# A two-layer decoder trunk: a wider stationary operand in the block MLP, and the DeltaNet coupling product cut to its 64x64 chunk

## The chip, the cores and the metric

One core of one Trainium2 chip. The metric is device microseconds of the whole program, the median over runs. Engines are named as the profile names them: PE is TensorE (PEld its weight loads, which run beside it), DVE is VectorE, ACT is ScalarE, POOL is GpSimd, and SP is SyncE, whose queue issues most DMAs. A product here is one matmul call of the kernel: `out = lhsT.T @ rhs`, with `lhsT` the stationary operand (loaded into the array) and `rhs` the moving one.

## The reference, cut to what matters

The reference is a trunk of two layers on 256 tokens of width 2048, batch 1. Layer 0 mixes tokens with NSA attention and retention, layer 1 with a gated DeltaNet; both go on with cross-attention into 256 memory tokens and a SwiGLU FFN. The change touches two places.

In layer 0, keys and values of NSA's compressed branch come from an MLP over overlapping blocks of 32 tokens (15 blocks, two groups):

```python
def compress_blocks(t, pos, w1, w2):
    ...
    blocks = blocks + pos[None, None, :, None, :].astype(t.dtype)
    flat = blocks.transpose(0, 3, 1, 2, 4).reshape(b, g, n_cmp, NSA_CMP_LEN * dh)
    return jax.nn.silu(flat @ w1) @ w2
```

`flat` has 30 rows (15 blocks by 2 groups) of 32 times 128 values, `w1` is 4096 by 256, `w2` is 256 by 128. It is done twice, for keys and for values.

In layer 1, each of 32 heads solves a unit lower triangular system per chunk of 64 tokens, and the state passes from chunk to chunk:

```python
def chunk_gated_delta_rule(q, k, v, beta, g):
    ...
    lower = jnp.where(strict, jnp.einsum('bhncd,bhnmd->bhncm', kb, k) * decay, 0.0)
    ...
    sol = lax.linalg.triangular_solve(lower + jnp.eye(C, dtype=f32), rhs, left_side=True,
                                      lower=True, unit_diagonal=True)
```

## The kernel before, in words

**Exact products from two parts.** The large products don't run in plain fp32. Weights and activations are each split into a high part (rounded to the fp32r type by a copy on ScalarE) and a low part (the rest, by a subtraction on VectorE), and three products with fp32r operands are added up: high by high, high by low, low by high (`passes`, line 232). A weight tile of 512 KB is loaded by SP into one of four buffers (`load_weight`, line 218) and split in pieces of 512 columns by lines 214 and 215. The products of all projections and of the block MLP are issued from line 237.

**Order of the work.** The kernel is one straight program. Projections run in the foreground; everything else (attention heads, the block MLP, the triangular inverses, the solves) are generator tasks. After every six products of a projection a counter advances by one (`tick`, line 112), and each task whose waiting time is over issues its next piece; `yield n` waits `2 n` ticks. So the interleaving is written out by hand in the number of projection products between two pieces of a task. The tile framework then fixes each engine's order once, ahead of the run.

**The block MLP** (`compress`, line 858, spawned twice by `nsa_keys`, for keys and values). It adds the position terms to windows of the projected tokens (tile `cf`), splits the result into `cfh` and `cfl` of 32 by 30 columns, and then for each of the 32 token positions multiplies by that position's 128 rows of `w1`: the 30 columns are stationary, 256 weight columns move, three products per position, 96 per branch, into 30 partitions of one PSUM bank (`cmp`). Both branches run between the products of the NSA query projections, so that SP's queue brings one tile of projection weights and two of block weights in turn. Afterwards silu is taken on the 30 partitions (three activations and a multiplication), two transposes (line 888) turn it, two copies (line 891) bring it to SBUF, and the second layer follows (lines 895 and 906).

**The DeltaNet solves** (`solver`, line 1383; `pair` and `head` in it, spawned by `gdn_inputs` for 16 key heads with two value heads each). The inverses of all 64x64 triangles are worked out ahead (`invert`, line 1311), go through DRAM by 16 stores of SP (line 1355), and come back by `pair` (line 1398) as block-diagonal tiles `bd` of 128 by 128: two chunks of 64 tokens at once, in two buffers that are filled with zeros once (line 1387). With 256 tokens a head has two such halves, t = 0 and 1. In `head`:

- `M` holds the decayed key scores of both halves and between them; `bv` holds beta times v.
- Line 1437, two products per head: the transposed inverses times the scores within a half, 128 by 128 times 128 by 128, give the coupling of the second chunk to the first; one copy on ScalarE (line 1439) puts both halves into the tile `nT`. `clear` (in `gdn_inputs`) has set the scores within a half to zero but for rows 0 to 63 and columns 64 to 127, so the result is zero outside that block.
- Line 1448, per half: `nT` (stationary) times `bv` (moving), which VectorE subtracts with a decay factor (line 1449); line 1451: the inverses times the result; line 1452: a copy to `u`. Line 1445 couples the halves.
- Lines 1454 to 1456 form the output; it is normalised and gated into `nT` again (line 1465), transposed (line 1470) and stored in `R` (line 1474).

All these products have plain fp32 operands. They run in between projections of values and the output projection, by the same ticks (`HOP` is 1).

Of the kernel before, what the change touches and what calls it, by code (L numbers as in the profile page):

```python
# [10 lines left out]
F32 = mybir.dt.float32  # L11
F32R = mybir.dt.float32r
AF = mybir.ActivationFunctionType
ALU = mybir.AluOpType
# [4 lines left out]
P = 128  # L19
# [59 lines left out]
def trunk(ctx: ExitStack, tc: tile.TileContext, a: dict, out: bass.AP, phases=ALL):  # L79
    nc = tc.nc  # L80
    V, S, G, PE = nc.vector, nc.scalar, nc.gpsimd, nc.tensor
# [55 lines left out]
    def give(n):  # L137
        state["banks"] += n
# [6 lines left out]
    ident = gp.tile([P, P], F32, name="ident")  # L145
# [72 lines left out]
    def load_weight(W, k0, nk, c0, ncol, g=None):  # L218

        w = wp.tile([P, nk, ncol], F32, tag="w", name="w")  # L220
        state["load"] = nc.sync.dma_start(w, W[k0 * P : (k0 + nk) * P, c0 : c0 + ncol].rearrange("(k p) c -> p k c", p=P))
        n = max(1, 512 // ncol)
        parts = []
        if g is not None:
            n = 1
        for k in range(0, nk, n):
            m = min(n, nk - k)
            h, l = split_weight(w[:, k : k + m, :], g and g(k0 + k))
            parts += [(h[:, i, :], l[:, i, :]) for i in range(m)]
        return parts  # L230

    def passes(o, x, w, start, last, x_stationary=False):

        (xh, xl), (h, l) = x, w
        pairs = ((xh, h), (xh, l), (xl, h)) if x_stationary else ((h, xh), (h, xl), (l, xh))
        for j, (s_, m) in enumerate(pairs):
            PE.matmul(o, s_, m, start=start and j == 0, stop=last and j == 2, skip_group_check=True)  # L237
# [153 lines left out]
    def sigmoid_(dst, src):  # L391

        S.activation(dst, src, AF.Exp, scale=-1.0)
        S.activation(dst, dst, AF.Ln, bias=c_one[: dst.shape[0]])
        S.activation(dst, dst, AF.Exp, scale=-1.0)
# [462 lines left out]
    def compress(ck, br, kvT, kcat, vc):  # L858

        f = ck.tile([P, 32, 30], F32, tag="cf", name="cf")  # L860
        for g in range(2):
            src = kvT[:, 2 * br + g, :]
            win = bass.AP(src.tensor, src.offset, [list(src.ap[0]), [1, 32], [16, 15]])
            pos = small[:, 17 + 32 * br : 17 + 32 * (br + 1)]
            V.tensor_add(f[:, :, g * 15 : (g + 1) * 15], win, pos[:, :, None].to_broadcast([P, 32, 15]))
        fh = ck.tile([P, 32, 30], F32R, tag="cfh", name="cfh", bufs=2)
        fl = ck.tile([P, 32, 30], F32R, tag="cfl", name="cfl", bufs=2)
        S.activation(fh, f, AF.Copy)
        V.tensor_sub(fl, f, fh.bitcast(F32))
        w2 = ck.tile([P, 2, P], F32, tag="cw2", name="cw2", bufs=2)  # L870
        S.dma_start(w2, a["nsa_cmp_w2"][0, br].rearrange("(j p) c -> p j c", p=P))
        W1 = a["nsa_cmp_w1"][0, br]
        yield from take(1)
        b = bank("cmp")
        ph = b[:30, 0:256]
        for k0 in range(0, 32, 4):
            for k, w in enumerate(load_weight(W1, k0, 4, 0, 256)):
                kk = k0 + k
                passes(ph, (fh[:, kk, :], fl[:, kk, :]), w, kk == 0, kk == 31, True)
                if k % 2:  # L880
                    yield 1
        sg = ck.tile([30, 256], F32, tag="csg", name="csg", bufs=2)
        hs = ck.tile([30, 256], F32, tag="chs", name="chs", bufs=2)
        sigmoid_(sg, ph)
        V.tensor_mul(hs, ph, sg)
        yield 2
        for j in range(2):
            PE.transpose(b[:, 256 + j * 32 : 256 + j * 32 + 30], hs[:, j * P : (j + 1) * P], ident[:30, :30])
        hT = ck.tile([P, 2, 30], F32, tag="chT", name="chT", bufs=2)
        for j in range(2):  # L890
            V.tensor_copy(hT[:, j, :], b[:, 256 + j * 32 : 256 + j * 32 + 30])
        yield 1
        if br == 0:
            for j in range(2):
                PE.matmul(b[:, 0:30], w2[:, j, :], hT[:, j, :], start=j == 0, stop=j == 1)
            kr = ck.tile([P, 30], F32, name="kr")
            V.tensor_copy(kr, b[:, 0:30])
            give(1)
            kn = ck.tile([P, 30], F32, name="kn")
            yield from head_rms(kr, kg[:, 0:1], kn, n=30)  # L900
            for g in range(2):
                V.tensor_copy(kcat[:, g, 512:527], kn[:, g * 15 : (g + 1) * 15])
        else:
            for g in range(2):
                for j in range(2):
                    PE.matmul(
                        b[:15, g * P : (g + 1) * P], hT[:, j, g * 15 : (g + 1) * 15], w2[:, j, :],
                        start=j == 0 and g == 0, stop=j == 1, skip_group_check=True,
                    )
                V.tensor_copy(vc[:15, g, :], b[:15, g * P : (g + 1) * P])  # L910
            give(1)
# [471 lines left out]
    def solver(gs, R, d_T, d_rows, neg, colD, beta, negc, rq, mhalf):  # L1383

        bds = [gs.tile([P, 2, 2, 2, P], F32, name=f"bd{j}", bufs=1) for j in range(2)]
        for bd in bds:
            G.memset(bd, 0.0)
        gcol = small[:, 16:17]

        def pair(q, vT, z, before):  # L1390
# [20 lines left out]
        def head(h, j, vT, z, bd, gb, begun):  # L1411
            yield from take(1)
            q = h // 2
            m = gs.tile([P, 384], F32, tag="M", name="M")
# [9 lines left out]
            b = bank("slv")  # L1424
            zc = (h % 4) * P
# [8 lines left out]
                S.activation(bv[:, t, :], b[:, 256 + t * P : 256 + (t + 1) * P], AF.Copy, scale=col(beta, t))  # L1434
            yield 1
            for t in range(2):
                PE.matmul(b[:, t * P : (t + 1) * P], bd[:, j, t, 0, :], m[:, 2 * t * P : 2 * t * P + P], start=True, stop=True)  # L1437
            nT = gs.tile([P, 2, P], F32, tag="nT", name="nT")
            S.activation(nT, b[:, 0:256].rearrange("p (t c) -> p t c", t=2), AF.Copy)
            yield HOP  # L1440
            u = gs.tile([P, 2, P], F32, tag="u", name="u")
            for t in range(2):
                rhs = bv[:, t, :]
                if t:
                    PE.matmul(b[:, 0:P], m[:, P:256], u[:, 0, :], start=True, stop=True)  # L1445
                    V.scalar_tensor_tensor(rhs, b[:, 0:P], col(negc, 1), rhs, ALU.mult, ALU.add)
                    yield HOP
                PE.matmul(b[:, 256:384], nT[:, t, :], rhs, start=True, stop=True)  # L1448
                V.scalar_tensor_tensor(rhs, b[:, 256:384], col(negc, t), rhs, ALU.mult, ALU.add)
                yield HOP  # L1450
                PE.matmul(b[:, 384:512], bd[:, j, t, 1, :], rhs, start=True, stop=True)  # L1451
                S.activation(u[:, t, :], b[:, 384:512], AF.Copy)
                yield HOP
# [9 lines left out]
            V.tensor_mul(st[:, 2:4], st[:, 2:4], rq[:, :, h])  # L1463
            for t in range(2):
                V.scalar_tensor_tensor(
                    nT[:, t, :], b[:, t * P : (t + 1) * P], st[:, 2 + t : 3 + t], z[:, t, zc : zc + P], ALU.mult, ALU.mult
                )
            yield 2 * HOP
            for t in range(2):
                PE.transpose(b[:, 256 + t * P : 256 + (t + 1) * P], nT[:, t, :], ident)  # L1470

            while len(begun) < 2:
                yield 1
# [53 lines left out]
```

## Time and profile before

| | |
|---|---|
| time, median of 3 runs | 3032.07 us (3030.87 to 3035.57) |
| the profiled execution | 3029.89 us |
| its span, first to last instruction | 3028.1 us |
| PE busy | 2962.2 us (98%), 22981 products' records |
| PEld busy | 2839.1 us (94%) |
| DVE busy | 2034.9 us (67%) |
| ACT busy | 1698.0 us (56%) |
| POOL busy | 111.9 us (4%) |
| DMA | 568.56 MB, mean 188 GB/s |
| PE's granted clock, mean | 0.991 |

Times are microseconds from the span's start unless marked ns. PE's records are pipelined: a product's duration reaches into the next one's, so what a product costs is read from the distance of starts, not from its duration. A row of the timeline gives start, length, engine, line, operation, `out<-in`, the shape, and how many instructions are merged into it; `30*128` means 30 rows (partitions of the contraction) by 128 columns of the stationary operand, `128x256` what moves. In brackets stands idle time of that engine ahead of the row and who ended it; "issue" is a release that the profile doesn't show.

### The profile page before, as it was taken

To read this page: it belongs to the slowest core of one execution; us is meant where nothing else is said; L and a number is where in the kernel's file an instruction comes from. 1 tells how busy PE (TensorE), PEld (TensorE's weight loads), DVE (VectorE), ACT (ScalarE), POOL (GpSimd) and SP (SyncE) were. 2 spreads that over 40 slices of the span, in tenths; PEclk is the share of its full clock that TensorE was granted. 3 is DMA by queue.
4 is the path that set the end of the run, shared out by engine and by line. 5 is a ranking of instruction groups with operands and counts; after the bars stand their busy time and mean duration, and the time that the engine had idled before them with its cause. 6 is when DMAs were issued, how large, how long until landed. Compare 5 with 4: busy or idle time off the path is not lost.

```text
span 3028.1 us, 59625 instructions
## 1 busy us (share of the span) xinstructions
PE 2962.2 (98%) x22981; PEld 2839.1 (94%) x22981; DVE 2034.9 (67%) x3879; ACT 1698.0 (56%) x3316; POOL 111.9 (4%) x153
## 2 busy tenths in 40 slices
PE   9999999999999999999989959999999999999999
PEld 8899899999999999999978959999999999999887
DVE  6867676675666665567689948886667566655554
ACT  6655655665555554456655637776556554545444
POOL 0000000000000000000110100122000000000000
PEclk9999999999999999999999989999999999999999
DMA  7775555566666665566777557564556666665664
GB/s 242 204 235 168 154 147 174 181 182 195 193 196 190 195 195 195 195 196 183 195 223 229 173 145 200 164 173 132 192 183 182 194 194 190 187 188 182 199 197 167
DMA packets 339547, 568.56 MB, mean 188 GB/s; under 512 B 43661, under 2 KB 83653, under 8 KB 339133
## 3 DMA queue, kind: packets, MB, share of 16 engines
q1 hardware_dynamic: 333376, 550.79, 61.2%
q0 software_dynamic: 2576, 7.82, 0.9%
q10 hardware_dynamic: 3308, 6.14, 0.7%
q8 instruction: 180, 2.95, 0.4%
q14 instruction: 107, 0.87, 0.1%
HBM read 549.16 MB, written 13.93 MB: 186 GB/s over the span
## 4 chain that ended last, share of the span: by engine, by line
PE 95%; DVE 2%; DMA 2%; SPq 1%; ACT 1%; issue 0%; POOL 0%; DVEq 0%; ACTq 0%; POOLq 0%
PE pj L237 87%; SPq L1355 1%; PE cmp L237 1%; DMA w<-in_hyb_w_in 1%; DVE w_lo L215 1%; PE slv L1451 0%; PE slv L1448 0%; PE slv L1437 0%; DMA w<-in_gdn_w_in 0%; DVE xT L424 0%; DMA d_T<-AB 0%; DVE x_lo L357 0%; PE slv L1445 0%; DMA mraw<-in_mem 0%; PE kk L1065 0%
## 5 line engine op out<-in xcount | busy, mean ns | idle before, releaser
L215 DVE TENSOR_TENSOR w_lo<-w,w_hi 128x512 fp32r<-128x512 f32 x1938 | 1329.6, 692 | 862.7 <-ACT w_hi L214 847.6
L214 ACT ACTIVATE w_hi<-w 128x512 fp32r<-128x512 f32 x1938 | 1217.1, 631 | 1141.0 <-DVE w_lo L215 589.8
L237 PE MATMUL pj<-x_hi,w_hi 128*128 128x256 f32 (+1 forms) x4496 | 1247.0, 280 | 36.5 <-ACT w_hi L214 36.1
L237 PE MATMUL pj<-x_lo,w_hi 128*128 128x256 f32 x4496 | 1246.1, 279 | 0.0
L237 PE MATMUL pj<-x_hi,w_lo 128*128 128x256 f32 (+1 forms) x4496 | 1226.0, 280 | 1.2 <-DVE w_lo L215 1.2
L237 PEld LDWEIGHTS pj<-x_hi,w_hi 128*128 128x128 f32 (+1 forms) x4496 | 848.2, 189 | 39.2 <-ACT w_hi L214 37.5
L237 PEld LDWEIGHTS pj<-x_lo,w_hi 128*128 128x128 f32 x4496 | 845.2, 188 | 1.1 <-issue 0.2
L237 PEld LDWEIGHTS pj<-x_hi,w_lo 128*128 128x128 f32 (+1 forms) x4496 | 831.4, 188 | 3.0 <-DVE w_lo L215 2.2
L237 PE MATMUL pj<-hl,w_hi 128*128 128x256 f32 x704 | 193.7, 276 | 0.0
L237 PE MATMUL pj<-hh,w_hi 128*128 128x256 f32 x704 | 193.6, 276 | 0.0
L237 PE MATMUL pj<-hh,w_lo 128*128 128x256 f32 x704 | 192.4, 276 | 0.0
L237 PE MATMUL pj<-o,w_hi 128*128 128x256 f32 x1024 | 184.8, 283 | 2.0 <-ACT o L1007 1.6
L237 PE MATMUL pj<-w_lo,x_hi 128*128 128x512 f32 (+2 forms) x448 | 172.1, 385 | 3.5 <-DVE w_lo L215 3.5
L237 PE MATMUL pj<-w_hi,x_lo 128*128 128x512 f32 (+2 forms) x448 | 169.5, 379 | 0.0
L237 PEld LDWEIGHTS pj<-o,w_hi 128*128 128x128 f32 x1024 | 157.3, 191 | 2.8 <-ACT o L1007 2.1
L237 PE MATMUL pj<-w_hi,x_hi 128*128 128x512 f32 (+2 forms) x448 | 142.6, 384 | 4.4 <-ACT w_hi L214 4.4
L237 PE MATMUL pj<-o,w_lo 128*128 128x256 f32 x512 | 142.3, 282 | 0.0
L237 PE MATMUL pj<-w_hi,hl 128*128 128x512 f32 x352 | 138.3, 393 | 0.0
L237 PE MATMUL pj<-w_lo,hh 128*128 128x512 f32 x352 | 137.7, 391 | 0.0
L237 PEld LDWEIGHTS pj<-hl,w_hi 128*128 128x128 f32 x704 | 132.2, 188 | 0.0
L237 PEld LDWEIGHTS pj<-hh,w_hi 128*128 128x128 f32 x704 | 132.2, 188 | 0.0
L237 PEld LDWEIGHTS pj<-hh,w_lo 128*128 128x128 f32 x704 | 131.3, 188 | 0.0
(414 smaller groups left out, 3621.7 us busy)
## 6 DMA issues: line engine op xcount, KB each, us to landing
w<-in_ffn_w_in SPq DMA_DIRECT2D x352, 512.0 KB
w<-in_gdn_w_in SPq DMA_DIRECT2D x193, 512.0 KB
w<-in_ffn_w_out SPq DMA_DIRECT2D x176, 512.0 KB
w<-in_hyb_w_in SPq DMA_DIRECT2D x96, 512.0 KB
w<-in_gdn_w_out SPq DMA_DIRECT2D x64, 512.0 KB
w<-in_xa_wkv SPq DMA_DIRECT2D x32, 512.0 KB
w<-in_hyb_w_out SPq DMA_DIRECT2D x32, 512.0 KB
w<-in_nsa_cmp_w SPq DMA_DIRECT2D x16, 512.0 KB
```

What stands on the lines that cost most here:

```text
L214: state["hi"] = S.activation(h, w, AF.Copy)
L215: V.tensor_sub(l, w, h.bitcast(F32))
L237: PE.matmul(o, s_, m, start=start and j == 0, stop=last and j == 2, skip_group_check=True)
L1355: nc.sync.dma_start(bass.AP(dst.tensor, dst.offset, [[64 * 512, 8], [512, 64], [1, 128]]), AB[p0 : p0 + 15 : 2].rearrange("p i w j -> p i ...
```

## The change

The block MLP puts high and low part side by side into one tile `cfp` of 60 columns per position. One product with the high weights then does both parts at once (60 partitions of PSUM), and one of 30 columns with the low weights adds to the first 30: two products per position instead of three. The two halves of the result are added only after the transposes, and silu is taken there, on 128 partitions by 60 elements. The evacuation is reordered with it.

In the solves, the coupling product takes only the 64 rows and 64 columns that matter: the first chunk's inverse and the scores from the first chunk to the second. Its result goes into columns 64 to 127 of one of four fixed tiles `ns` of 64 partitions, filled with zeros once; the product with it (line 1448) contracts over 64 partitions instead of 128. The tile `nT` is gone; the gated output goes into `bv`.

```diff
@@ -863,33 +863,35 @@
             win = bass.AP(src.tensor, src.offset, [list(src.ap[0]), [1, 32], [16, 15]])
             pos = small[:, 17 + 32 * br : 17 + 32 * (br + 1)]
             V.tensor_add(f[:, :, g * 15 : (g + 1) * 15], win, pos[:, :, None].to_broadcast([P, 32, 15]))
-        fh = ck.tile([P, 32, 30], F32R, tag="cfh", name="cfh", bufs=2)
-        fl = ck.tile([P, 32, 30], F32R, tag="cfl", name="cfl", bufs=2)
-        S.activation(fh, f, AF.Copy)
-        V.tensor_sub(fl, f, fh.bitcast(F32))
+
+        fp = ck.tile([P, 32, 60], F32R, tag="cfp", name="cfp", bufs=2)
+        S.activation(fp[:, :, 0:30], f, AF.Copy)
+        V.tensor_sub(fp[:, :, 30:60], f, fp.bitcast(F32)[:, :, 0:30])
         w2 = ck.tile([P, 2, P], F32, tag="cw2", name="cw2", bufs=2)
         S.dma_start(w2, a["nsa_cmp_w2"][0, br].rearrange("(j p) c -> p j c", p=P))
         W1 = a["nsa_cmp_w1"][0, br]
         yield from take(1)
         b = bank("cmp")
-        ph = b[:30, 0:256]
         for k0 in range(0, 32, 4):
-            for k, w in enumerate(load_weight(W1, k0, 4, 0, 256)):
+            for k, (h, l) in enumerate(load_weight(W1, k0, 4, 0, 256)):
                 kk = k0 + k
-                passes(ph, (fh[:, kk, :], fl[:, kk, :]), w, kk == 0, kk == 31, True)
+                PE.matmul(b[:60, 0:256], fp[:, kk, :], h, start=kk == 0, stop=kk == 31, skip_group_check=True)
+                PE.matmul(b[:30, 0:256], fp[:, kk, 0:30], l, start=False, stop=kk == 31, skip_group_check=True)
                 if k % 2:
                     yield 1
-        sg = ck.tile([30, 256], F32, tag="csg", name="csg", bufs=2)
-        hs = ck.tile([30, 256], F32, tag="chs", name="chs", bufs=2)
-        sigmoid_(sg, ph)
-        V.tensor_mul(hs, ph, sg)
+        hs = ck.tile([60, 256], F32, tag="chs", name="chs", bufs=2)
+        S.activation(hs, b[:60, 0:256], AF.Copy)
+        yield 1
+        for j in range(2):
+            PE.transpose(b[:, 256 + j * 64 : 256 + j * 64 + 60], hs[:, j * P : (j + 1) * P], ident[:60, :60])
+        bt = b[:, 256:384].rearrange("p (j c) -> p j c", j=2)
+        hT = ck.tile([P, 2, 30], F32, tag="chT", name="chT", bufs=2)
+        sg = ck.tile([P, 2, 30], F32, tag="csg", name="csg", bufs=2)
+        V.tensor_copy(hT, bt[:, :, 0:30])
+        V.tensor_add(hT, hT, bt[:, :, 30:60])
+        sigmoid_(sg, hT)
+        V.tensor_mul(hT, hT, sg)
         yield 2
-        for j in range(2):
-            PE.transpose(b[:, 256 + j * 32 : 256 + j * 32 + 30], hs[:, j * P : (j + 1) * P], ident[:30, :30])
-        hT = ck.tile([P, 2, 30], F32, tag="chT", name="chT", bufs=2)
-        for j in range(2):
-            V.tensor_copy(hT[:, j, :], b[:, 256 + j * 32 : 256 + j * 32 + 30])
-        yield 1
         if br == 0:
             for j in range(2):
                 PE.matmul(b[:, 0:30], w2[:, j, :], hT[:, j, :], start=j == 0, stop=j == 1)
@@ -1385,6 +1387,10 @@
         bds = [gs.tile([P, 2, 2, 2, P], F32, name=f"bd{j}", bufs=1) for j in range(2)]
         for bd in bds:
             G.memset(bd, 0.0)
+
+        ns = [gs.tile([64, 2, P], F32, name=f"ns{j}", bufs=1) for j in range(4)]
+        for n in ns:
+            G.memset(n, 0.0)
         gcol = small[:, 16:17]
 
         def pair(q, vT, z, before):
@@ -1434,9 +1440,12 @@
                 S.activation(bv[:, t, :], b[:, 256 + t * P : 256 + (t + 1) * P], AF.Copy, scale=col(beta, t))
             yield 1
             for t in range(2):
-                PE.matmul(b[:, t * P : (t + 1) * P], bd[:, j, t, 0, :], m[:, 2 * t * P : 2 * t * P + P], start=True, stop=True)
-            nT = gs.tile([P, 2, P], F32, tag="nT", name="nT")
-            S.activation(nT, b[:, 0:256].rearrange("p (t c) -> p t c", t=2), AF.Copy)
+                PE.matmul(
+                    b[0:64, t * 64 : (t + 1) * 64], bd[0:64, j, t, 0, 0:64], m[0:64, 2 * t * P + 64 : 2 * t * P + P],
+                    start=True, stop=True,
+                )
+            n = ns[h % 4]
+            S.activation(n[:, :, 64:128], b[0:64, 0:128].rearrange("p (t c) -> p t c", t=2), AF.Copy)
             yield HOP
             u = gs.tile([P, 2, P], F32, tag="u", name="u")
             for t in range(2):
@@ -1445,7 +1454,7 @@
                     PE.matmul(b[:, 0:P], m[:, P:256], u[:, 0, :], start=True, stop=True)
                     V.scalar_tensor_tensor(rhs, b[:, 0:P], col(negc, 1), rhs, ALU.mult, ALU.add)
                     yield HOP
-                PE.matmul(b[:, 256:384], nT[:, t, :], rhs, start=True, stop=True)
+                PE.matmul(b[:, 256:384], n[:, t, :], rhs[0:64, :], start=True, stop=True)
                 V.scalar_tensor_tensor(rhs, b[:, 256:384], col(negc, t), rhs, ALU.mult, ALU.add)
                 yield HOP
                 PE.matmul(b[:, 384:512], bd[:, j, t, 1, :], rhs, start=True, stop=True)
@@ -1463,11 +1472,11 @@
             V.tensor_mul(st[:, 2:4], st[:, 2:4], rq[:, :, h])
             for t in range(2):
                 V.scalar_tensor_tensor(
-                    nT[:, t, :], b[:, t * P : (t + 1) * P], st[:, 2 + t : 3 + t], z[:, t, zc : zc + P], ALU.mult, ALU.mult
+                    bv[:, t, :], b[:, t * P : (t + 1) * P], st[:, 2 + t : 3 + t], z[:, t, zc : zc + P], ALU.mult, ALU.mult
                 )
             yield 2 * HOP
             for t in range(2):
-                PE.transpose(b[:, 256 + t * P : 256 + (t + 1) * P], nT[:, t, :], ident)
+                PE.transpose(b[:, 256 + t * P : 256 + (t + 1) * P], bv[:, t, :], ident)
 
             while len(begun) < 2:
                 yield 1
```

## Rows read from the trace of the kernel before

**Rows 1.** The page, chain that ended last, by engine.
```profile
PE 95%; DVE 2%; DMA 2%; SPq 1%; ACT 1%; issue 0%; POOL 0%; DVEq 0%; ACTq 0%; POOLq 0%
```

**Rows 2.** Table of stretches, block MLP: length, busy (count) per engine, clock, DMA share, GB/s.
```profile
200.00:210.00 10.00, 10.00 (x88) 9.55 (x87) 7.81 (x14) 6.35 (x11) 0.00 (x0) 1.00 0.93 293
...
220.00:232.50 12.50, 12.50 (x110) 11.92 (x109) 8.91 (x15) 9.65 (x19) 0.00 (x0) 1.00 0.91 289
```

**Rows 3.** Block products, one kind: ns min/median/max, first and last start, forms.
```profile
L237 PE MATMUL cmp<-w_hi,cfh x64: 276/278/285, 187.8 to 232.1; 128*30 128x256 f32 x64
```

**Rows 4.** Chain of waits, block MLP: start us, us, what, count.
```profile
202.05 2.10 PE cmp L237 x18
```

**Rows 5.** Waits, 180 to 255 us: total us, times, longest.
```profile
ACT w_hi L214 <- DMA w<-in_hyb_w_in: 3.3, 3, 2.2
```

**Rows 6.** Table of stretches, DeltaNet stage.
```profile
1840.00:1900.00 60.00, 60.00 (x523) 60.00 (x522) 52.34 (x139) 44.72 (x120) 10.67 (x16) 1.00 0.63 172
...
2020.00:2100.00 80.00, 76.20 (x645) 74.25 (x644) 60.34 (x156) 56.83 (x165) 19.45 (x28) 0.99 0.49 135
```

**Rows 7.** Timeline of TensorE in the block MLP: start us, us, what.
```profile
201.53 0.28 PE L237 MATMUL pj<-x_lo,w_hi 128*128 128x256 f32 x1
201.65 0.28 PE L237 MATMUL cmp<-w_hi,cfh 128*30 128x256 f32 x1
201.77 0.28 PE L237 MATMUL pj<-x_hi,w_lo 128*128 128x256 f32 x1
```

**Rows 8.** Products of the solves, lines 1437 and 1448.
```profile
L1437 PE MATMUL slv<-M,bd x128: 270/275/275, 1829.1 to 2086.7; 128*128 128x128 f32 x128
...
L1448 PE MATMUL slv<-bv,nT x128: 270/274/343, 1832.0 to 2090.9; 128*128 128x128 f32 x128
```

**Rows 9.** Timeline of TensorE around one product of line 1448.
```profile
1834.67 0.28 PE L237 MATMUL pj<-x_lo,w_hi 128*128 128x256 f32 x1
1834.79 0.39 PE L1448 MATMUL slv<-bv,nT 128*128 128x128 f32 x2
1834.93 0.36 PE L237 MATMUL pj<-x_hi,w_lo 128*128 128x256 f32 x1
1835.13 0.28 PE L237 MATMUL pj<-x_hi,w_hi 128*128 128x256 f32 x1
```

**Rows 10.** Timeline of TensorE and its weight loads before transposes over 30 partitions.
```profile
238.80 0.28 PE L237 MATMUL pj<-x_lo,w_hi 128*128 128x256 f32 x1
...
239.01 0.20 PEld L888 LDWEIGHTS cmp<-ident,chs 30*128 30x128 f32 x2
```

**Rows 11.** The same behind transposes over 64 partitions.
```profile
1396.29 0.33 PE L1140 MATMUL g<-ident,wr 64*128 64x64 f32 x2 [0.24 <-DVE wr L1135]
1396.55 0.19 PEld L237 LDWEIGHTS pj<-x_hi,w_hi 128*128 128x128 f32 x1
...
1396.77 0.28 PE L237 MATMUL pj<-x_lo,w_hi 128*128 128x256 f32 x1
```

**Rows 12.** Weight loads before a product over 33 partitions [idle before, releaser].
```profile
104.92 0.09 PEld L741 LDWEIGHTS g<-ohs,rbt 33*8 33x8 f32 x2 [0.33 <-issue]
```

**Rows 13.** Timeline of TensorE around a transpose over 81 partitions.
```profile
27.55 0.28 PE L237 MATMUL pj<-ml,w_hi 128*128 128x256 f32 x1
27.67 0.23 PE L185 MATMUL g<-ident,s 81*128 81x81 f32 x1
...
27.90 0.28 PE L237 MATMUL pj<-mh,w_hi 128*128 128x256 f32 x1
```

**Rows 14.** Four weight loads of 128 columns.
```profile
242.41 0.53 PEld L895 LDWEIGHTS cmp<-chT,cw 128*128 128x128 f32 x4
```

**Rows 15.** Chain of waits near the end of the solves: start us, us, what.
```profile
2085.59 1.34 PE slv L1437 x12
...
2087.16 0.96 PE slv L1448 x8
```

**Rows 16.** GpSimd, the zero fills of line 1387.
```profile
1813.86 1.84 POOL L1387 MEMSET bd<- 128x1024 f32 x2 [67.99 <-DMA w<-in_gdn_w_in]
```

## The prediction

> **What bounds the kernel now.** I read the chain of waits on the page first: 95% of the span lies on TensorE, so whatever shortens or lengthens TensorE's own stream counts, and work on other engines counts only where TensorE runs out of operands [rows 1]. Then I read the table of stretches for the two places that the change touches.
>
> In the block MLP stretch TensorE is busy in all of each slice, but the 16 DMA engines are too, at 0.93 and 0.91 of their time and 293 and 289 GB/s [rows 2]. The reader is to see two limits lying almost on each other. The 192 block products (three kinds, 64 each) start between 187.8 and 232.1 us [rows 3], and 18 in a row on the chain take 2.10 us, 0.117 us each [rows 4]. In the same stretch ScalarE, which splits each weight tile, waited 3.3 us in three places for a weight load to land [rows 5].
>
> In the DeltaNet stretch TensorE is busy for 60.0 us of 60 and then 76.2 of 80 [rows 6]: there is almost no idle time to hide anything in before the very last heads. DMA is at 0.63 and 0.49 there and is no limit. The 1% that the chain gives to SP's stores of the solved triangles lies ahead of this stage; what waits for them (the first beta-v tiles, and the weight splits queued behind them on ScalarE) waits as before.
>
> **Part 1, the block MLP.** The change leaves out one product in three: 64 of 192, at 0.117 us, is 7.5 us of TensorE. The 60-column operand costs no more than the 30-column one as far as rows show: projections (128 columns) and block products (30) alternate at 0.12 us whatever the width of the operand [rows 7], because the 256 moving columns are the same. That is the whole gain if nothing else binds. But the bytes stay. At a DMA share of about 0.92 the 44.3 us from first to last product could shrink only to 0.92 of that before the queues are full all the time, a gain of 3.5 us. The share is no exact ceiling, since it counts the time that packets take and not what the queues could carry, so I take 4.5 us, nearer to the DMA bound than to 7.5. Below, as little as 0 if the loads already land just in time, and above, 7.5.
>
> The rest of this part I cost at nothing. The subtraction that makes the low half must now be done before the first product instead of the third: two products, 0.23 us, of a wait that shows no idle time now. The evacuation is reordered (a copy and transposes first, then the sigmoid on 60 elements per partition instead of 256, so shorter instructions), and the hand-written yields add up to the same three steps; the projections that TensorE does meanwhile hide it. If that cover were gone it would cost about a microsecond once per branch. No DMA is added or moved, and SP's queue keeps its order.
>
> **Part 2, the DeltaNet solves.** There are 32 heads with two coupling products and two products with their result; each product shows as two records, 128 records per line [rows 8]. In the stream as it is, such a pair costs only its place: from the projection before it to the second one after it 0.46 us pass, of which two projection intervals are 0.23, so 0.225 us per pair and 0.112 us per record [rows 9].
>
> The coupling product now moves 64 columns instead of 128. Taken alone that halves it: 128 records by 0.057 us, 7.3 us saved. The product after it keeps 128 stationary and 128 moving columns and saves nothing.
>
> But both now contract over 64 partitions. What TensorE does when it goes from products over 128 partitions to a short one and back is in the trace, and this is where I put the weight. Before the 30-partition transposes the next weight load starts 0.21 us after the last projection instead of at once [rows 10]: 0.09 us beyond the projection's own 0.12, and the load is no longer hidden. Behind the 64-partition transposes, the load, the two records and the gap behind them take 0.26 us up to the next projection's load, and that projection's successor comes 0.22 us after this load instead of 0.117, so its load of 0.11 us is exposed [rows 11]. Of the 0.26 us, 0.09 is the same stop and 0.17 is a load and two records of 64 columns, about 0.055 us each. An ordinary product, over 33 partitions, also has 0.33 us of idle weight loading ahead of it that no wait explains [rows 12], though a part of it is the longer product before. Against that, a transpose over 81 partitions passes without a stop: 0.35 us from projection to second projection, which is two intervals and one record [rows 13]. So 64 partitions are on the stopping side, 81 are not.
>
> [...]
>
> Worked out per group. Coupling pair of one head, four records: stop 0.09, load 0.055, four records 0.22, stop 0.09, exposed projection load 0.11, together 0.565 against 0.45 now: +0.115 us, times 32, +3.7 us. Product with the result, two records: stop 0.09, load of 128 columns 0.11 (four such loads back to back take 0.53 us, the last being 0.19 long, so 0.11 apart [rows 14]), two records 0.225, stop 0.09, exposed load 0.11, together 0.625 against 0.225: +0.40 us, times 64, +25.6 us. That is 29.3 us. Some groups stand next to each other: near the end 12 coupling records follow in one run (three heads) and 8 of the other (four products) [rows 15], which share one entry and exit; that takes off about 2 us, and about 2 more fall into the 3.8 us that TensorE idles late in this stage [rows 6]. Sum: +25 us. Lower bound +10, if the loads are hidden after all and only two stops of 0.09 us are paid in each of 96 groups (17.3 us, less the 7.3 saved); upper +29.
>
> The rest goes together at nothing: four zero fills more on GpSimd behind two that take 1.84 us for four times the elements per partition [rows 16], about a microsecond, at 1816 us, 13 us before the first coupling product [rows 8]; a smaller copy on ScalarE; the gated output in the beta-v tile instead of the old result tile, which has as many buffers and whose next user, four heads later, begins only after this pair is done. If the fills were late, ScalarE's copy and the weight splits behind it would wait for that microsecond.
>
> **Sum.** The profiled execution took 3029.89 us, 2.2 us under the median of 3032.07. 3029.9 - 4.5 + 25 = 3050.4 us; on the median's level 3052.5 us.
>
> **Rivals.** (a) No stop: the short products are issued like the narrow operands of the block MLP [rows 7]. For it: those narrow operands, which use only part of the array too; against it: [rows 10 to 12], where partitions change. Then 7.3 us and 4.5 us are saved: 3020 us, faster. It decides as soon as the stops and exposed loads come to under 0.12 us per group. [...] (b) Only the coupling product, short in both dimensions, is stopped, and the one with 128 stationary columns runs as before: +3.7 - 4.5, 3031 us, no change. For it, the transposes of [rows 10, 11] are not ordinary products; against it, they too have 128 stationary columns. (c) The stop comes as I say, but the loads hide in it and the block MLP gives its full 7.5 us: +10 - 7.5, 3034.5 us, hardly to be told from no change; it is the lower end of my own case.
>
> **How the numbers follow.** A measurement of this kernel can tell about 0.2%, 6 us. My case 0.86, (a) 0.08, (b) 0.06. Within my case the time runs from 3034.5 (c) to 3032 + 29 - 0 = 3061. I give 3036 to 3061: it leaves out (a), (b) and the outer edge of mine. Faster 0.08, same 0.06, slower 0.86.
>
> **What would show it.** In the changed profile: 128 block products instead of 192, with a first-to-last stretch of some 40 us, a DMA share near 1.0 and more ScalarE waits for block weights. In the DeltaNet stage: weight loads of both lines starting about 0.2 us behind the product before them, the next projection's successor 0.22 us on, fewer records per 60 us at the same full busy share (some 480 instead of 523), and no new waits on other engines. If the loads of the 64-partition products start at once behind the product before them, my prediction is wrong and (a) or (b) holds; if the DeltaNet stage is longer by waits on ScalarE or VectorE instead, its cause is wrong.

## The result, and the profile after

The changed kernel takes 3061.90 us (median of 5 runs, 3055.83 to 3068.23), the kernel before 3033.08 us (5 runs beside it): a ratio of 1.0095, with an interval of 1.008 to 1.011. That is slower, as forecast; the time lies 9.4 us over the one forecast and 0.9 us above the range. The profiled execution after took 3055.83 us (span 3054.1), 25.9 us more than the one before, and 6 us under its own median.

First the page of the changed kernel, the chain that ended last by engine, which answers to [rows 1].

```profile
PE 93%; DMA 2%; DVE 2%; SPq 1%; ACT 1%; issue 0%; POOL 0%; DVEq 0%; ACTq 0%; POOLq 0%
```

TensorE is still the bound: no new engine has taken over. Then the table of stretches, for the block MLP and the DeltaNet stage, against [rows 2, 6] (length, busy time and count for PE, PEld, DVE, ACT and POOL, granted clock, DMA share, GB/s).

```profile
200.00:210.00 10.00, 8.40 (x70) 7.99 (x71) 8.09 (x16) 6.27 (x13) 0.00 (x0) 1.00 0.91 275
220.00:232.50 12.50, 11.69 (x91) 9.96 (x90) 8.90 (x15) 9.00 (x19) 0.00 (x0) 1.00 0.95 296
...
1840.00:1900.00 60.00, 60.00 (x482) 56.17 (x481) 48.55 (x125) 40.45 (x110) 8.83 (x16) 1.00 0.60 165
2020.00:2100.00 80.00, 76.45 (x579) 70.12 (x578) 57.75 (x139) 50.76 (x134) 15.96 (x20) 0.96 0.47 144
```

Two different things are to be seen. In the block MLP TensorE, which had no idle time before, now has 1.60 us of it in 10. In the solves it is as busy as it was, 60.00 of 60, and yet issues 482 products in place of 523 (the prediction had some 480): time goes inside the stream, and a busy share doesn't show it. The products and the timeline do. First the products of both places by line, against [rows 3, 8] (ns min/median/max, first and last start, forms).

```profile
L878 PE MATMUL cmp<-w_hi,cfp x64: 274/279/469, 190.0 to 231.4; 128*60 128x256 f32 x64
L879 PE MATMUL cmp<-w_lo,cfp x64: 276/279/469, 190.6 to 231.6; 128*30 128x256 f32 x64
...
L1443 PE MATMUL slv<-M,bd x128: 217/218/268, 1825.8 to 2113.6; 64*64 64x64 f32 x128
L1457 PE MATMUL slv<-bv,ns x128: 271/272/374, 1828.3 to 2118.5; 64*128 64x128 f32 x128
```

The 128 block products need 41.6 us (190.0 to 231.6), the 192 before 44.5. ScalarE's waits for block weights grew, as forecast, from 1.0 us in one place to 3.3 in five; the DMA share, 0.91 and 0.95, did not come near 1.0 as forecast. Next the timeline of PE and its weight loads around one product with the coupling's result, against [rows 9].

```profile
1833.79 0.28 PE L237 MATMUL pj<-x_hi,w_lo 128*128 128x256 f32 x1
1833.99 0.29 PEld L1457 LDWEIGHTS slv<-bv,ns 64*128 64x128 f32 x2
1833.99 0.49 PE L1457 MATMUL slv<-bv,ns 64*128 64x128 f32 x2
1834.41 0.19 PEld L237 LDWEIGHTS pj<-x_hi,w_hi 128*128 128x128 f32 x1
1834.41 0.38 PE L237 MATMUL pj<-x_hi,w_hi 128*128 128x256 f32 x1
...
1834.63 0.28 PE L237 MATMUL pj<-x_lo,w_hi 128*128 128x256 f32 x1
```

From the projection before to the second one after, 0.84 us pass where 0.46 passed [rows 9]: 0.20 to the load (0.12 is ordinary), 0.42 for load, two records and the way out, and 0.22 until the next projection's successor, because that projection's own load is no longer hidden (load and product both start at 1834.41). These are the three pieces that the prediction priced. The median over all places of this kind (a "group" from here on: the time from the projection ahead of some products of the solves to the second projection behind them) is 0.845 us (36 of them; 0.459 before, 40); for the coupling pair it is 0.804 (14; 0.682 before, 18). So the stops cost, all told, 0.386 and 0.122 us per group, 64 x 0.386 + 32 x 0.122 = 28.6 us.

One more place is new, late in the solves (table of stretches).

```profile
2024.00:2028.00 4.00, 3.61 (x27) 2.85 (x25) 3.42 (x11) 3.71 (x10) 2.37 (x4) 1.00 0.47 137
2028.00:2032.00 4.00, 0.84 (x5) 0.45 (x4) 4.00 (x8) 4.00 (x10) 3.67 (x3) 0.76 0.18 56
2032.00:2036.00 4.00, 4.00 (x20) 4.00 (x21) 4.00 (x8) 1.47 (x4) 2.53 (x2) 0.50 0.62 212
2036.00:2040.00 4.00, 4.00 (x32) 3.80 (x31) 3.66 (x9) 3.30 (x9) 0.00 (x0) 0.88 0.13 36
```

TensorE idles 3.2 of the 4 us from 2028 us (among others for `split_heads`, VectorE's `o` of line 1010, ahead of the output projection), and then its granted clock stands at 0.50 for the next 4 us: 20 products, against 37 from 2020 to 2024 us. Before, the same place had 0.9 us of idle time in 8 and a clock of 1.00 throughout:

```profile
2014.00:2018.00 4.00, 3.50 (x31) 3.26 (x30) 3.69 (x9) 3.96 (x11) 0.00 (x0) 1.00 0.72 219
2018.00:2022.00 4.00, 3.63 (x31) 3.44 (x31) 4.00 (x6) 4.00 (x10) 3.64 (x3) 1.00 0.54 182
```

Taken from the first projection of the stage to the last product of the solves, the stage grew from 281.6 to 311.9 us, 30.3 us.

### The profile page after: what moved, and what is told of

It is laid out like the page before. It is cut to its first block, busy times and chain, and to the rows that moved or that the text cites. A ratio compares the mean times of both kernels' runs of the same rounds, so it can differ in the third digit from the quotient of the medians.

```text
span 3054.1 us, 59537 instructions
## 1 busy us (share of the span) xinstructions
PE 2984.0 (98%) x22917; PEld 2839.8 (93%) x22917; DVE 2036.2 (67%) x3879; ACT 1695.8 (56%) x3318; POOL 108.4 (4%) x157
## 4 chain that ended last, share of the span: by engine, by line
PE 93%; DMA 2%; DVE 2%; SPq 1%; ACT 1%; issue 0%; POOL 0%; DVEq 0%; ACTq 0%; POOLq 0%
PE pj L237 86%; SPq L1357 1%; PE slv L1457 1%; DVE w_lo L215 1%; DMA w<-in_hyb_w_in 1%; DMA w<-in_gdn_w_in 1%; DMA w<-in_nsa_cmp_w 1%; PE slv L1460 0%; PE slv L1443 0%; DVE xT L424 0%; ACT w_hi L214 0%; DMA d_T<-AB 0%; PE slv L1454 0%; DVE x_lo L357 0%; DMA mraw<-in_mem 0%
```

## The experiments

Every ratio is against the kernel before, run beside it on the same chip. Prices of groups are medians. A "sequence" is the order that the framework has fixed for each engine's instructions. The code is shown by the lines that make the point; the zero-filled tiles `ns` and the copy into them follow in size.

**Halves of the change: e1 to e4.** e1 has the new block MLP and the old solves; e2 the old block MLP and the new solves; e3 and e4 have the old block MLP and one short product each (against e2):

```diff
 e3: the product with the result over all 128 partitions
-PE.matmul(b[:, 256:384], n[:, t, :], rhs[0:64, :], start=True, stop=True)
+PE.matmul(b[:, 256:384], n[:, t, :], rhs, start=True, stop=True)
 e4: the coupling product in full, 128x128 by 128
-b[0:64, t * 64 : (t + 1) * 64], bd[0:64, j, t, 0, 0:64], m[0:64, 2 * t * P + 64 : 2 * t * P + P],
+b[:, t * P : (t + 1) * P], bd[:, j, t, 0, :], m[:, 2 * t * P : 2 * t * P + P],
```

> The block MLP as changed, the solves as before. Theory: one product in three is gone (7.5 us of TensorE), but the block weights come no faster, so about 4 us are gained in the stretch and nothing is lost later: 4 us less than before. Rival 1, TensorE alone sets this stretch: 7.5 us less. Rival 2, the loads already land just in time: within 1 us of before, and then the whole of the change's loss is smaller than the solves alone make it.

> The solves as changed, the block MLP as before. Theory (each run of products over 64 partitions stops TensorE at its beginning and end): 28.6 us from the two group prices read in the changed kernel's profile (0.122 us for 32 coupling groups, 0.386 us for 64 products with the result), and a little for a new order of instructions near the end: 28 to 33 us more than before. Rival, the two parts of the change disturb each other: clearly under 25 us.

> Only the coupling product is cut to 64 by 64; its result goes into zero-filled tiles of 128 partitions, and the product with it contracts over 128 partitions as before. Theory of the stops: 32 groups at 0.122 us, about 4 us more than before, with starts of the coupling product 0.2 us behind the projection before it. Rival, no price for a change of shape: 7 us less. Rival, the loss comes from the fixed tiles, their zero fills or the new order: 20 us more or above, since all of that is here too.

> The coupling product is as before (128 by 128), and only the product with its result contracts over 64 partitions. Theory of the stops: 64 groups at 0.386 us, 24.7 us, plus up to 5 us if the order near the end changes: 24 to 30 us more than before. Rival, the coupling product carries the loss: under 10 us. Together with the run before, the two should add up to the solves alone.

Measured: e1 3031.78 us, ratio 1.0001 [0.9989, 1.0012]; e2 3073.79, 1.0137 [1.0124, 1.0150]; e3 3048.42, 1.0049 [1.0034, 1.0064]; e4 3055.92, 1.0078 [1.0065, 1.0091]; before 3032.83. The solves carry the whole loss. e1's time can't be told from before's, but it is not the block MLP's alone: e1's DeltaNet stage, with the solves of before, took 285.0 us against 281.6, in another sequence. It idles 5.9 us against 3.9 and has a stretch at the lower clock (table of stretches of e1):

```profile
2016.00:2020.00 4.00, 2.06 (x14) 1.36 (x13) 4.00 (x13) 3.89 (x9) 3.52 (x4) 1.00 0.27 85
2020.00:2024.00 4.00, 3.27 (x16) 3.04 (x16) 4.00 (x8) 3.83 (x9) 4.00 (x4) 0.58 0.67 185
```

e4, with groups of 0.847 us, lies 23.1 us over before by the medians, just under the 24 to 30 expected, and 24.8 by its groups. But e2 lies 41.0 us over it, where 28 to 33 were expected, and e3, whose coupling groups cost 0.808 us and its other groups 0.459 as before, 15.6 us where its stops make 4. So e2 and e3 share some 12 us that no group shows, and e2 minus e3, 25.4 us, is just the price of the 64 products over 64 partitions. PE, DVE, ACT and SP carry the same instructions in the same sequence in e2 and e3; it differs from before's and from the changed kernel's. The table of stretches of e3 near the end of the solves shows what it does.

```profile
2096.00:2100.00 4.00, 0.78 (x5) 0.48 (x5) 3.61 (x12) 1.54 (x8) 3.50 (x7) 0.93 0.95 242
2100.00:2105.00 5.00, 5.00 (x25) 3.71 (x25) 1.56 (x6) 3.87 (x12) 0.06 (x1) 0.50 0.00 0
2105.00:2110.00 5.00, 5.00 (x28) 4.54 (x27) 1.40 (x4) 1.54 (x6) 0.00 (x0) 0.53 0.00 0
```

In this sequence the last heads' output products stand together, and TensorE waits 3.2 us ahead of them; the ten microseconds behind that run at a clock of 0.50 to 0.53. In all, e3's TensorE is idle 10.7 us in the stage (gaps between starts of over 0.6 us, less 0.2 each) against 3.9 before. The granted clock, summed in slices of 2 us, takes some 7 us from 2026 to 2032 and 2098 to 2110 us; before has no low clock in the stage but for its first 6 us and its end. The stage can be added up start by start: the distance to the next start, less the median of its kind before, goes to the stops if it is under 0.6 us at full clock, to the idle time if it is longer, and to the clock where that was at 0.50. Of the 15.2 us by which e3's stage is longer, 2.6 are stops, 7.1 idle time and 5.5 clock. e2 shows the same with a dip over 22 us:

```profile
2110.00:2118.00 8.00, 4.78 (x41) 4.36 (x40) 6.39 (x17) 4.61 (x21) 4.41 (x8) 1.00 0.78 197
2118.00:2140.00 22.00, 21.47 (x92) 17.51 (x90) 6.19 (x20) 8.78 (x32) 1.46 (x5) 0.53 0.00 1
```

**Which dimension stops TensorE: e5, e6, e9.** All have the old block MLP and the fixed tiles `ns`; e5 and e6 keep the product with the result over 128 partitions. The lines are the operands of the coupling product, and for e9 the product with its result.

```diff
 e5: 128 partitions, 64 stationary columns
+b[0:64, t * 64 : (t + 1) * 64], bd[:, j, t, 0, 0:64], m[:, 2 * t * P + 64 : 2 * t * P + P],
 e6: 128 partitions, 128 stationary columns, 64 moving
+b[:, t * 64 : (t + 1) * 64], bd[:, j, t, 0, :], m[:, 2 * t * P + 64 : 2 * t * P + P],
 e9: 96 partitions, 96 stationary columns; the result's product over 96 partitions
+b[0:96, t * 64 : (t + 1) * 64], bd[0:96, j, t, 0, 0:96], m[0:96, 2 * t * P + 64 : 2 * t * P + P],
+PE.matmul(b[:, 256:384], n[:, t, :], rhs[0:96, :], start=True, stop=True)
```

> Before's block MLP; coupling product over all 128 partitions with 64 stationary and 64 moving columns, product with the result over all 128 partitions. PE, DVE, ACT and SP carry the same instructions in the same sequence as in e3_square_only. Theory (the number of partitions is what stops TensorE, the number of columns does not): no stops; the group of two coupling products between projections falls from 0.808 us in e3 to about 0.46 (half the columns of before's 0.68, projection included), so 32 x 0.35 = 11 us less than e3, about 3037. What is still over before is then the order alone. Rival (64 columns stop it too): the group stays at 0.80 and the time at e3's 3048.

> Before's block MLP; coupling product with its full 128x128 stationary operand and 64 moving columns, product with the result over 128 partitions. Theory: no stops, 0.22 us less for each of 32 groups of two coupling products, so 7 us less than before (3026) where the framework's order leaves the tail without projections as it was; up to 11 us more than that (3037) where it draws the heads together near the end as in e3. Rival (moving columns below 128 also stop TensorE): a group price of 0.68 or more and a time at or above before's 3033.

> Before's block MLP; the solves of e2_solves_only with 96 partitions and 96 columns in place of 64 (rows 64 to 95 of the operands are zeros or meet zeros). Theory (64 or fewer partitions or fp32 columns stop TensorE, 96 do not, as the transpose of 81 rows did not): the groups cost what they cost before, 0.68 us for two coupling products and 0.46 for the pair of products with the result, projection included, against 0.80 and 0.846 in e2; time at before's 3034, or up to 7 us over it where the order draws idle time into the tail as in e2. Rival (anything less than the full array stops it): groups of 0.80 and 0.85 and some 3060 to 3074.

Measured: e5 3048.38 us, 1.0047 [1.0031, 1.0063]; e6 3035.26, 1.0002 [0.9992, 1.0013]; e9 3035.51, 1.0010 [1.0001, 1.0019]. The timelines of PE around a coupling pair, e5 first:

```profile
1833.69 0.28 PE L237 MATMUL pj<-x_lo,w_hi 128*128 128x256 f32 x1
1833.89 0.45 PE L1441 MATMUL slv<-M,bd 128*64 128x64 f32 x4
1834.27 0.38 PE L237 MATMUL pj<-x_hi,w_hi 128*128 128x256 f32 x1
1834.49 0.28 PE L237 MATMUL pj<-x_lo,w_hi 128*128 128x256 f32 x1
```

e6:

```profile
1833.22 0.28 PE L237 MATMUL pj<-x_lo,w_hi 128*128 128x256 f32 x1
1833.34 0.56 PE L1441 MATMUL slv<-M,bd 128*128 128x64 f32 x4
1833.70 0.36 PE L237 MATMUL pj<-x_hi,w_hi 128*128 128x256 f32 x1
1833.91 0.28 PE L237 MATMUL pj<-x_lo,w_hi 128*128 128x256 f32 x1
```

e9:

```profile
1832.06 0.28 PE L237 MATMUL pj<-x_lo,w_hi 128*128 128x256 f32 x1
1832.18 0.47 PE L1441 MATMUL slv<-M,bd 96*96 96x64 f32 x4
1832.47 0.36 PE L237 MATMUL pj<-x_hi,w_hi 128*128 128x256 f32 x1
1832.67 0.28 PE L237 MATMUL pj<-x_lo,w_hi 128*128 128x256 f32 x1
```

e5 fell on the rival's side: with all 128 partitions and 64 fp32 columns the first record still starts 0.20 us behind the projection instead of 0.12, the projection behind still pays 0.22 us, the group is at 0.808 us and the time is e3's (the sequence is e3's too). So 64 stationary fp32 columns stop TensorE as 64 partitions do. e9 has no stop (0.606 and 0.462 us), as the 81 rows of [rows 13] had none, and lies 2.3 us over before by the medians, with 7.7 us of idle time in the stage against 3.9. e6 has the group price that its rival named, but not its stop (the first record starts 0.12 us behind the projection): 64 moving columns behind a full stationary operand cost 0.683 us per group, as 128 moving did, so the 7 us are not there, while 96 stationary columns cost 0.606. The starts of these records lie 0.059 us apart (medians) with 64 stationary columns (e5), 0.083 with 96 and 0.111 with 128, with 64 columns moving each time. Other fp32 products of the trace before show that the moving columns count where they are more: 15 stationary and 128 moving 0.109 us (line 906), 128 and 1 0.112 (line 336), 128 and 256 0.216 (line 582). In these rows the pace goes by the larger of the two numbers. In e9 the product with the result, 96 rows by 128 columns, cost 0.462 us per group (0.459 over 128 rows), and the coupling product, 96 rows by 96 columns, 0.606 (0.683 in e6 with 128 by 128 and the same 64 moving): between 128 and 96 the price went by the stationary columns and not by the rows.

**Per switch or per product: e8.** e2 with each product of the short kind issued twice in a row.

```diff
+for _ in range(2):
+    PE.matmul(b[:, 256:384], n[:, t, :], rhs[0:64, :], start=True, stop=True)
```

> As e2_solves_only, but each product with the coupling's result over 64 partitions is issued twice in a row; 64 more products. Theory (the stop is paid at the switch between 128 and 64 partitions, not by the product): the second product costs its own 0.22 us, 64 x 0.22 = 14 us over e2 (3088), and the group of a product's records between two projections grows from 0.845 by 0.22. Rival (every product over 64 partitions stops by itself): the group grows by 0.6, 64 x 0.6 = 39 us over e2 (3112). The order near the end differs from e2's, so the group decides before the time does.

The timeline of PE in e8:

```profile
1834.48 0.28 PE L237 MATMUL pj<-x_hi,w_hi 128*128 128x256 f32 x1
1834.69 0.71 PE L1456 MATMUL slv<-bv,ns 64*128 64x128 f32 x4
1835.33 0.38 PE L237 MATMUL pj<-x_hi,w_lo 128*128 128x256 f32 x1
1835.55 0.29 PE L237 MATMUL pj<-x_hi,w_hi 128*128 128x256 f32 x1
```

The group's median is 1.065 us, 0.22 over 0.845: the second product costs itself and no stop, so the stop belongs to the switch. The time missed: 3071.78 us (1.0127 [1.0107, 1.0147]) where 3088 was expected, 2 us under e2's although 14 us of work were added. Its sequence is a new one, with 4.8 us of idle time in the stage and no low clock but for the stage's first 6 us and its end. So short products alone don't bring the 12 us that e2 loses beyond its stops; e2, e3 and e5, which share a sequence, all show such a loss (e5 some 10 us).

**What holds the block MLP: e10, e11.** Both load one tile of block weights and use it for all positions; e10 has the three products of before, e11 the two of the change.

```diff
+w0 = state["w0"]
-for k, w in enumerate(load_weight(W1, k0, 4, 0, 256)):
+for k, w in enumerate(load_weight(W1, k0, 4, 0, 256, w=w0)):
```

> Before's solves and before's block MLP with three products per position, but the block weights of the first four positions are loaded once and stand in for all (14 of 16 tiles of 512 KB are not loaded; the block MLP's values change with that). Theory (in before, the loads were the nearest limit of this stretch): the block MLP gets shorter by itself, since the projection's tiles come without waiting, and is now bound by products: from the 100th to the 260th splitting copy under 230 us where before took 232.3, DMA share far below 0.9 at 200 to 230 us. Rival (products bound it before too): the stretch stays at 232 to 233 us.

> The same stand-in weights with the changed block MLP (two products per position) and before's solves. Theory (the third products came free beside the loads): without the loads the whole of 64 x 0.117 = 7.5 us shows between e10 and this, from the 100th to the 260th splitting copy, against about 2 us between the kernels with loads (233.0 against 231.1). Rival (something other than the loads took the gain, for instance the splitting copies on ScalarE or the counters that pace the pieces): the difference stays at 2 us or less.

Block products of e10, one of three kinds, then of e11:

```profile
L238 PE MATMUL cmp<-w_hi,cfh x64: 274/278/283, 192.2 to 236.5; 128*30 128x256 f32 x64
```

```profile
L883 PE MATMUL cmp<-w_hi,cfp x64: 274/279/469, 191.9 to 229.8; 128*60 128x256 f32 x64
L884 PE MATMUL cmp<-w_lo,cfp x64: 276/279/469, 192.5 to 229.9; 128*30 128x256 f32 x64
```

e10 shows the rival right for the kernel before: without loads its block products take 44.6 us, as with them (44.5), and from the 100th to the 260th splitting copy (ScalarE's copies that make the high parts of weights) 232.3 us pass, again as before. TensorE alone bound that stretch. e11 takes 38.0 us, and from the first block product to the end of the second layer 51.5 against 59.0: the whole 7.5 us are there once the loads are gone (5.9 from the 100th to the 260th copy). With the loads, the two-product form took 41.6 us in the changed kernel, 45.7 in e1, 42.7 in e7 and 43.8 in e12. By the median e11 gains 3.0 us, 0.9990 [0.9981, 0.9999], e10 nothing, 1.0001 [0.9992, 1.0011]. e11's other 4.5 us went in the DeltaNet stage: with the solves of before it took 286.1 us against 281.6 (281.2 in e10), again in another sequence. Where e1's block MLP loses what it gained is in its table of stretches:

```profile
204.00:206.00 2.00, 0.71 (x6) 0.41 (x5) 1.69 (x4) 0.07 (x1) 0.00 (x0) 1.00 1.00 282
206.00:208.00 2.00, 0.19 (x2) 0.19 (x3) 0.21 (x1) 0.87 (x2) 0.00 (x0) 1.00 0.79 264
208.00:210.00 2.00, 2.00 (x12) 2.00 (x12) 1.09 (x2) 0.71 (x2) 0.00 (x0) 0.54 0.50 173
210.00:212.00 2.00, 2.00 (x13) 1.99 (x13) 0.69 (x1) 0.25 (x2) 0.00 (x0) 0.61 0.76 260
212.00:214.00 2.00, 2.00 (x20) 1.93 (x19) 1.38 (x3) 2.00 (x4) 0.00 (x0) 1.00 0.03 11
```

and one row of its timeline in that stretch, with the wait of ScalarE behind it (total us, times, longest):

```profile
207.81 0.33 PE L878 MATMUL cmp<-w_hi,cfp 128*60 128x256 f32 x1 [3.11 <-ACT w_hi L214]
...
ACT w_hi L214 <- DMA w<-in_nsa_cmp_w: 3.1, 1, 3.1
```

TensorE has caught up with the loads (DMA share 1.00), waits 3.11 us for one split tile, and then issues 12 and 13 products in 2 us in place of 20, at a mean granted clock of 0.54 and 0.61.

**Versions without stops: e7, e12.** e7 has the solves of e6, e12 those of e9, both with the new block MLP.

> The solves of e6_half_moving with the changed block MLP. Theory (the MLP's third products lay beside its loads, as e1 says): within 3 us of e6, but for another order near the end. Rival (the MLP gives its 4 us): 4 us under e6.

> The whole change, with 96 partitions and 96 columns in place of 64 in the solves. Theory: no stops, so the 28 us are gone; what is left is the block MLP's gain (0 to 4 us by the traces so far) against the idle time of the new order (up to 4 us): 3030 to 3036, no difference from before that can be measured. Rival (something else of the whole change costs time, as the fixed tiles or the block MLP's new evacuation): more than 3040.

Measured: e7 3031.95 us, 0.9999 [0.9988, 1.0011], 3.3 us under e6 and so between its two forecasts; e12 3035.23, 1.0010 [1.0000, 1.0020]. e12 is the whole change with 96 in place of 64, and the 28.8 us are gone. Its gap ahead of the output projection is there as in the changed kernel (4.6 us idle from 2010 to 2024 us, and a clock of 0.62 from 2016 to 2024), and in e1, which has the solves of before, too; so that gap is not the stops' doing. In other sequences (before, e4, e6) the waits at that place are shorter (0.9, 0.9 and 0.8 us of idle time) and no low clock follows (1.00). No version beats the kernel before.

## Why the prediction was right in direction and short in size

**The bound** held: the chain stayed on TensorE [rows 1], and no other engine became the limit, but for the waits late in the solves (below).

**The stops** held as a mechanism and as a price. Forecast were +0.40 us for each product with the result and +0.115 for each coupling pair; the groups show +0.386 and +0.122, 28.6 us where the prediction's own sum before deductions was 29.3. That TensorE stops at the switch is shown by e8 (1.065 us with two short products in a row, 0.845 with one), that 96 rows don't stop it by e9 (0.462 and 0.606 us per group) and e12 (ratio 1.0010). Rival (b) falls with e4, where the product with 128 stationary columns stops by itself, (c) with the exposed loads in the timeline, and (a) with both. The 7.3 us that the coupling product's records were to save are nearly there (their starts lie 0.059 us apart instead of 0.111), but not because 64 columns move: in e6 the moving columns alone are halved, and nothing is saved. The figure was right by luck, since both numbers fell to 64. One reading in the prediction was too narrow: it put the stop on the partitions alone ("against it: [rows 10 to 12], where partitions change"), and 64 fp32 columns over all 128 partitions stop TensorE too (e5, 0.808 us per group). The fp32r operands of the block MLP, of 30 columns [rows 7] and of 60 (0.12 us apart in the changed kernel), don't. The number 64 alone doesn't make the stop either, for in the trace before, projections with 64 fp32r columns stand between those of 128, 0.11 and 0.12 us apart:

```profile
1376.28 0.28 PE L237 MATMUL pj<-x_lo,w_hi 128*128 128x256 f32 x1
1376.39 0.28 PE L237 MATMUL pj<-x_hi,w_hi 128*64 128x256 f32 x1
1376.51 0.28 PE L237 MATMUL pj<-x_hi,w_lo 128*128 128x256 f32 x1
```

What TensorE does in the stop, and why fp32 operands bring it at 64 and not at 96, no run shows.

**The step that failed** is the pair of deductions from the solves' 29.3 us, and what they left out: "about 2 us" for neighbouring groups and "about 2 more" for idle time late in the stage. The first is there, and larger: a coupling pair right beside a product with the result costs 1.218 us (7 groups; 0.906 before), 0.2 less than both stops apart. Added up start by start as for e3, the stops come to 24.2 us in the stage, 4.4 under the 28.6 of groups that stand apart. The second has the wrong sign. Idle time late in the stage took up nothing; it grew, from 3.9 to 7.5 us, by waits on other engines that the prediction said would not be there, and a stretch of half clock stood behind it: 3.8 us for the idle time and 2.4 for the clock in the same sum. 24.2, 3.8 and 2.4 are the stage's 30.3 us but for rounding. So the solves were mis-sized by 5 us, +25 against +30. That the framework fixes a new sequence after an edit, worth from next to nothing (e4, e6, e8) through 3 to 5 us (e1, e11) to some 12 us (e2, e3), was in neither sum nor range. The sequence does it by itself: the same solves of before take 281.6 us and, in e1, 285.0, and the same new solves 311.9 in the changed kernel and 321.3 in e2.

**The block MLP** stays open. The two limits were read rightly as lying close together; e10 and e11 show that the first was TensorE and the second the loads. From the first block product to the end of the second layer the profiled executions took 59.0 us before and, in the two-product form with its loads, 55.1 (the changed kernel), 59.3 (e1), 56.2 (e7) and 57.5 (e12): gains of 3.9, none, 2.8 and 1.5 us. So the forecast of 4.5 lies above all four, and one lies at its lower bound of 0. By its medians e1 gains 1.0 us with a stage that is 3.4 us longer, which would leave 4 us for the block MLP in executions other than the profiled one; an interval of 3.5 us either way doesn't decide it. The forecast took the DMA share as a limit that is reached smoothly. What comes instead are single waits for a tile, up to 3.11 us, and the lower clock behind them (0.54 and 0.61 in e1).

**The balance.** Of the 25.9 us between the profiled executions, 30.3 lie in the stage and -4.4 elsewhere, where the prediction had +25 and -4.5: there the miss is the solves' alone. That the rest agrees so well is in part luck, since equal instructions scatter by more (the stage begins at 1816.6 us before and at 1822.8 in e3, with the same products ahead of it). By the medians 4 us more are missing. The prediction lifted its sum to the median's level by the 2.2 us of the kernel before, and the changed kernel's profiled execution lies 6.1 us under its median; where its other executions lose that is not seen.

## What to carry to other kernels

A short product that is interleaved one by one with full ones is paid at the switch, here 0.39 us for 0.22 us of work: pad it (96 rows cost 0.462 us per group, 128 rows 0.459) or issue the short ones one behind the other (0.22 us for the second in e8), before cutting rows or columns to 64. Where two limits lie close together, taking work from the first can expose the second as single waits: here up to 3.11 us, with a granted clock of 0.54 and 0.61 in the 4 us behind that one. A median that moves by 10 us after a small edit may be the new instruction sequence, and one that doesn't move can hide a gain and a loss (e11's 7.5 and 4.5 us): compare groups and stages in the trace before giving the edit the credit or the blame.

## What was unexpected of the hardware

- 64 stationary fp32 columns over all 128 partitions stop TensorE (0.808 us per group against 0.682), 96 by 96 don't (0.606), and fp32r operands of 60 or 64 columns beside 128 go at 0.11 to 0.12 us.
- Halving the moving columns of an fp32 product with a full stationary operand saved nothing (0.683 against 0.682 us); with 64 stationary columns as well the records start 0.059 us apart in place of 0.111.
- After TensorE had been mostly idle for 3 us (0.90 us busy in 4 in e1, 0.84 in 4 in the changed kernel, 0.78 in 4 in e3) its mean granted clock over the next 4 to 10 us was 0.50 to 0.61, though it was busy throughout; in e2, with 4.78 us busy in 8 and then only products of the solves, it was 0.53 over the next 22 us.
